# A hybrid RWKV7 / forgetting attention / delta net / differential attention block: score, value and low rank products as pairs of half-array products, and three orders of the out projection

## The chip, the cores and the metric

One core of a Trainium2 chip. The time is that of one execution on the device, in microseconds; of several executions the median is given. A profile is one further execution that the hardware profiler recorded. TensorE multiplies a stationary tile (loaded by a weight load, PEld in the profile) with a moving one (PE); VectorE (DVE), ScalarE (ACT) and GpSimd (POOL) work on vectors, and SyncE (SP) issues transfers.

## The reference, cut to what matters

512 tokens of 2048 features are normalised and multiplied by a wide input matrix. Four mixers of 1024 features each work on parts of the result; their outputs are gated and go through an out projection of 4096 x 2048.

```python
h = rms_norm(x, norm_g[l])
p = jnp.einsum('bsd,dn->bsn', h, w_in[l])
p_rwkv, p_fox, p_gdn, p_diff, z = jnp.split(p, bounds, axis=-1)
y = jnp.concatenate([rwkv7_time_mix(...), forgetting_attention(...),
                     gated_deltanet(...), differential_attention(...)], axis=-1)
x = x + jnp.einsum('bsm,md->bsd', y * jax.nn.silu(z), w_out[l])

# rwkv7_time_mix: the low rank products
w = (w0 + jnp.tanh(w_lo) @ w_up)                 # rank 64
a = jax.nn.sigmoid((a0 + a_lo @ a_up))           # rank 64
# forgetting_attention: 16 heads of 64, by blocks of 128 queries, causal
s = jnp.einsum('bhqd,bhkd->bhqk', q[:, :, q0:q0 + Q_BLOCK], k[:, :, :kv_end]) * scale
s = s + c[:, :, q0:q0 + Q_BLOCK, None] - c[:, :, None, :kv_end]
prob = softmax(where(distance >= 0, s, -inf))
o = jnp.einsum('bhqk,bhkd->bhqd', prob, v[:, :, :kv_end])
# differential_attention: 8 heads with two maps of 64 each, and values of 128
s = jnp.einsum('bhmqd,bhmkd->bhmqk', q[..., q0:q0 + Q_BLOCK, :], k[..., :kv_end, :]) * scale + alibi
weights = prob[:, :, 0] - lam * prob[:, :, 1]
o = jnp.einsum('bhqk,bhkd->bhqd', weights, v[:, :, :kv_end])
```

## The kernel before, in words

Large products are made from F32R parts: every operand is split into a large part and a small rest (`wh` and `wl`, `hh` and `hl`, `gh` and `gl`), and three products (large by large, rest by large, large by rest) add up in one PSUM bank. Smaller products that need full accuracy are F32, for which the trace has two records per product.

The kernel has these stages. First x is normalised, transposed and split (to about 50 us). Then eight steps j run, each on 128 features of every mixer: a stream of weight products (`gemm_fm`, `gemm_tm`, line 66 in the profile, tiles `acc_...`) is the filler, and between its products the mixers' own small products are set in. After the steps come the gate products (`acc_z`), and at the end the out projection (`acc_o`, from line 1394 on).

The order on TensorE is written out: each mixer is a generator (`rwkv_local`, `rwkv_chain`, `gdn`, `inverses`, `fox`, `diff`), and the loop at the end of the stages runs either the next product of the stream or the generator that is due, by an estimated clock `pe[0]`. `MM` (line 60) and `transpose` advance that clock; a generator yields the time that it wants to wait, stretched by `SLACK` = 1.25. `free(tag)` holds a generator back until the clock says that a PSUM bank is free again: `psc` hands out the two banks `sc` of the scores, `ptr` the one bank `tr` of the transposes, each with the time that it is planned to be held. TensorE runs that order strictly; the other engines are ordered by priorities. A bank or an operand that is late therefore stops all of TensorE.

The pieces that the change touches:

- `rwkv_local` (line 552): two F32R products per low rank part: `uh` by `lor` on 128 rows, where the two halves of the rows hold the large part and the rest of `lor`, and `ul` by `lor` on 64 rows. The order is 128 rows, 64, 128, 64, into the banks `pw` and `pa` (two of the tag `sc`).
- `qk_heads` (line 1046) normalises and transposes q and k of a pair of heads (fox) or of maps (diff) and writes three operands: `QS`, for each head both parts of q on the two halves of the rows, `KD`, for each head the large part of k on both halves, and `KL`, the rest of k. That takes six ScalarE and four VectorE instructions on 64 rows.
- `scores` (line 1080) makes per query block and head a 128-row product (QS by KD: large and rest of q with the large part of k in one go) and a 64-row product (QS's large part by KL), of 128, 256, 384 or 512 columns by block. The two heads have banks of their own (`pSf`, `pSd`). In fox a bf16 product with a mask follows per head. Then VectorE adds the bias and takes the maximum (line 1099), and ScalarE exponentiates (line 1101).
- `weighted` in `fox` (line 1140) transposes the weights of one head, copies them (line 1112), waits, and multiplies them with 64 columns of V in F32, into rows 0 to 63 (head 0) or 64 to 127 (head 1) of the bank `po`; then it does the same for the other head. `blocks` (line 1115) puts the scores of a block ahead of the value products of the block before, so that the next scores can follow directly on `po`.
- Two pieces that the change leaves alone show how small tiles run: `rwkv_local` makes `pA` (line 625) of 64-row F32 products, the two row halves in turn, into two banks; `inverses` makes `pm` (from line 1002 on) of products on 32 x 32 tiles, of which the third of each group reads the same rows as the first and writes other columns.
- The out projection: four column blocks `nb` of 512, each in 16 parts; per part 24 products into four banks, token block by token block, each with two groups of three products.

Of the kernel before, what the change touches and what calls it, by code (L numbers as in the profile page):

```python
# [39 lines left out]
# margin on the estimated latencies  # L40
# [11 lines left out]
def hybrid_kernel(ctx: ExitStack, tc: tile.TileContext, ins, out, steps=tuple(range(NJ)), ydbg=None, tail=True):  # L52
# [7 lines left out]
    def MM(o, a, b, **kw):  # L60
        n, m = math.prod(b.shape[1:]), math.prod(a.shape[1:])
        if a.dtype == F32:
            pe[0] += 4 * max(n, m, 32) / 2400
        else:
            pe[0] += max(n, 256 if a.dtype == F32R else 128) / 2400
        return nc.tensor.matmul(o, a, b, **kw)  # L66
# [26 lines left out]
    # banks by use, with the time at which each is expected to be free again  # L93
# [15 lines left out]
    def free(tag, n=1):  # L109
        """Wait until the next n banks are free."""  # L110
        while True:
            b = banks[tag]
            t = max(b[(taken[tag] + i) % len(b)] for i in range(n))
            if t <= pe[0]:
                return
            yield min(t - pe[0], 1.0)
# [6 lines left out]
    def until(*what):  # L123
        """Wait until another thread has come that far."""
        while what not in done:
            yield 0.5
# [18 lines left out]
    # ------------------------------------------------------------ constants  # L145
# [20 lines left out]
    # ------------------------------------------------------------ h = rms_norm(x), transposed, split  # L166
    # with the first product run block of tokens by block of tokens
# [108 lines left out]
    # key minus query position for the last block of queries, with the causal mask; halved for each pair of heads  # L276
# [13 lines left out]
    # ------------------------------------------------------------ streamed products  # L290
# [37 lines left out]
    def gemm_tm(ca, cb, name, evac, need, late=False):  # L328
        """Token-major; with late, the second bank is wanted late."""
# [29 lines left out]
    # ------------------------------------------------------------ low rank parts and gates  # L359
# [4 lines left out]
    # vectors along the features, put on the partitions  # L364
# [35 lines left out]
    # both parts of the low rank products on the two halves of the rows: of the decay's the large one first  # L400
# [33 lines left out]
    # gates: both parts of the weights beside each other  # L434
# [20 lines left out]
    def gates(fab0):  # L455
# [45 lines left out]
        # by block of 32 queries: the sums up to a key within the block, less those from a key up to the block  # L501
# [38 lines left out]
    # ------------------------------------------------------------ RWKV  # L540
# [11 lines left out]
    def rwkv_local(j, res, st):  # L552
# [6 lines left out]
        for i, ps in enumerate(pws):  # L559
            rs = slice(i * C, (i + 1) * C)  # L560
            MM(ps, uh[:, i], lor[i], start=True, stop=False)
            MM(ps, ul[rs], lor[i][rs], start=False, stop=True)
# [31 lines left out]
        # squared norms by token, their reciprocals as row scales  # L594
# [12 lines left out]
        # both halves of the chunks, each as soon as the step before is through with its tiles  # L607
# [3 lines left out]
        for q in range(2):  # L611
# [6 lines left out]
            # decayed interactions within a chunk  # L618
# [22 lines left out]
            # token-major copies  # L641
# [20 lines left out]
        # bonus  # L662
# [12 lines left out]
    def rwkv_chain(j, st, XT):  # L675
# [50 lines left out]
        # group norm by head, gain and offset after the transposition  # L726
# [23 lines left out]
    # ------------------------------------------------------------ gated delta net  # L750
# [12 lines left out]
    def gdn_silu(j, s, a):  # L763
        """Twice the function."""
# [18 lines left out]
    def gdn_local(j, res):  # L783
        # decays within a chunk
# [16 lines left out]
        # k: token-major, norms  # L801
# [24 lines left out]
        # q and the interactions  # L826
# [86 lines left out]
    # ------------------------------------------------------------ unit triangular inverses  # L913
    NB = 48

    def inverses(j, ET, GA, blk, start_rwkv):
# [42 lines left out]
        # the untransposed inverses of the leading blocks  # L959
# [8 lines left out]
        # RWKV: blocks of 32 into 64  # L968
# [16 lines left out]
        # delta net: 32 into 64  # L985
# [27 lines left out]
        # 64 into 128  # L1013
# [13 lines left out]
    # ------------------------------------------------------------ attentions  # L1027
# [18 lines left out]
    def qk_heads(j, ev, kind):  # L1046
# [10 lines left out]
        # by head: both parts of q on the two halves of the rows, the large part of k on both, and its small part  # L1057
        QS = mp.tile([P, 2, T], F32R, name=f"QS{kind}{j}", tag="QS", bufs=1)
        KD = mp.tile([P, 2, T], F32R, name=f"KD{kind}{j}", tag="KD", bufs=1)
        KL = mp.tile([P, T], F32R, name=f"KL{kind}{j}", tag="KL", bufs=1)  # L1060
        halves = slice(0, C), slice(C, P)
        for s, src in enumerate((qa, ka)):
            yield from free("tr")
            pt = ptr(f"pt{kind}{j}_{s}", 8.1)
            for t in range(NT):
                transpose(pt[:, t * P:(t + 1) * P], src[:, t, :])
            for h in range(2):
                hs, other = halves[h], halves[1 - h]
                g = gain[hs, gi + s:gi + s + 1]
                big = (QS, KD)[s][hs, h]  # L1070
                ACT(big, pt[hs], AF.Copy, scale=g)
                if s:
                    ACT(KD[other, h], pt[hs], AF.Copy, scale=g)
                STT(KL[hs] if s else QS[other, h], pt[hs], g, big.bitcast(F32), op0=ALU.mult, op1=ALU.subtract)
            yield 2.0
        yield 4.0
        done.add((kind + "_qk", j))
        return QS, KD, KL

    def scores(qk, qi, name, biases, masked):  # L1080
        """Both halves of a pair: exp of the scores less their maximum, and its sums."""
        QS, KD, KL = qk
        kv = (qi + 1) * P
        yield from free("sc", 2)
        pss = [psc(f"pS{name}_{h}", 3.5 + 0.5 * h) for h in range(2)]
        for h in range(2):
            hs = slice(h * C, (h + 1) * C)
            qs = slice(qi * P, (qi + 1) * P)
            MM(pss[h][:, 0:kv], QS[:, h, qs], KD[:, h, 0:kv], start=True, stop=False)
            MM(pss[h][:, 0:kv], QS[hs, h, qs], KL[hs, 0:kv], start=False, stop=masked)  # L1090
# [14 lines left out]
    def transposed(pr, qi, name):  # L1105
        """In its place."""
# [8 lines left out]
    def blocks(scored, weighted):  # L1115
        """All blocks of queries, the scores of one ahead of the products of the block before."""
# [8 lines left out]
    def fox(j, ev, values, nb):  # L1125
# [14 lines left out]
        def weighted(qi, res):  # L1140
            for h, (pr, _) in enumerate(res):
                yield from transposed(pr, qi, f"f{j}_{qi}_{h}")
                for kt in range(qi + 1):
                    MM(po[h * C:(h + 1) * C, qi * P:(qi + 1) * P], V[:, kt, h * C:(h + 1) * C],
                       pr[:, kt * P:(kt + 1) * P], start=(kt == 0), stop=(kt == qi))
# [56 lines left out]
    # ------------------------------------------------------------ all groups, in the order of an estimated clock  # L1202
# [26 lines left out]
    # those whose gates come in the first step, before their values  # L1229
# [127 lines left out]
    # ------------------------------------------------------------ gating  # L1357
    # the first half goes through DRAM, the second stays where the mixers were
# [35 lines left out]
    # ------------------------------------------------------------ out projection and residual  # L1394
# [6 lines left out]
    for nb in range(D // T):  # L1401
        cs = slice(nb * T, (nb + 1) * T)
        accs = [bank(tag, f"acc_o{nb}_{t}", 0.0) for t, tag in enumerate(sets[nb % 2])]
        for half in range(2):
            for q in halves[half]:
                for gp in (0, 2):
# [7 lines left out]
                    for t in range(NT):  # L1414
                        ts_ = slice(t * P, (t + 1) * P)
                        for g in range(2):
                            m = (gp + g) * NJ + q
                            sl = slice(g * T, (g + 1) * T)
                            MM(accs[t], gh[m][:, ts_], wh[:, sl], start=(first and g == 0), stop=False)
# [35 lines left out]
```

## Time and profile before

| | |
|---|---|
| three runs | 2347.38, 2352.05, 2352.88 us; median 2352.05 |
| span of the profiled execution | 2347.7 us |
| TensorE matmuls | busy 2326.0 us (99%), 14364 records |
| weight loads | busy 1939.0 us (83%) |
| VectorE, ScalarE, GpSimd | busy 1386.2 us (59%), 832.1 us (35%), 220.0 us (9%) |
| mean granted TensorE clock | 0.996 |
| mixers (50 to 1640 us) | 1590 us |
| last gate products (1640 to 1989.5 us) | 349.5 us |
| out projection (1989.5 to 2347.7 us) | 358.2 us |

The profiled execution's own span, 2347.7 us, lies within the three runs and 4.35 us below their median. Matmuls are pipelined and a record's end is modelled, so two records overlap and the sum of their durations is no use of time; what a product costs is read from its start to the start of the next one. In the timeline a row is one record or several alike that follow each other (xcount), with its start and its length; `64*128 64x512` is 64 rows by 128 columns of the array, fed 512 columns.

### The profile page before, as it was taken

The numbers are of one execution on the slowest core, as the hardware profiler recorded it, in microseconds if no ns is written. First come the engines' busy times: TensorE is split into PE (matmuls) and PEld (weight loads), VectorE is DVE, ScalarE is ACT, GpSimd is POOL, SyncE is SP. The second block draws the span as 40 slices with busy tenths as digits, with TensorE's granted clock in tenths as the row PEclk, the third lists the DMA queues.
The fourth block names the chain that finished last, engine by engine and source line by source line (L and its number), as shares of the span: only waits on it lengthen the run. The fifth ranks groups of instructions, "written<-read, shape, count | busy, mean of one in ns | idle before, by whom it ended". The sixth has DMA issues, their size and how long they took to land.

```text
span 2347.7 us, 36745 instructions
## 1 busy us (share of the span) xinstructions
PE 2326.0 (99%) x14364; PEld 1939.0 (83%) x14364; DVE 1386.2 (59%) x3585; ACT 832.1 (35%) x1456; POOL 220.0 (9%) x434
## 2 busy tenths in 40 slices
PE   7999999999999999999999999999999999999999
PEld 6788779779878977987987897798788888888887
DVE  6468487567757847756785784776553343422222
ACT  4234343344344334334434333443332222311111
POOL 2200020102102002010210201201000000100000
PEclk9999999999999999999999999999999999999999
DMA  5433223323322322332332232233354444654452
GB/s 162 101 87 99 81 62 97 88 58 94 97 61 66 102 80 54 104 84 58 99 89 64 69 99 75 60 97 87 96 161 135 129 112 110 175 132 108 117 125 72
DMA packets 320848, 225.78 MB, mean 96 GB/s; under 512 B 16911, under 2 KB 284370, under 8 KB 320162
## 3 DMA queue, kind: packets, MB, share of 16 engines
q1 hardware_dynamic: 298722, 187.05, 30.2%
q0 software_dynamic: 8128, 14.84, 3.1%
q10 hardware_dynamic: 13824, 21.54, 2.8%
q8 instruction: 113, 1.85, 0.3%
q14 instruction: 61, 0.50, 0.1%
HBM read 203.40 MB, written 19.97 MB: 95 GB/s over the span
## 4 chain that ended last, share of the span: by engine, by line
PE 98%; DVE 1%; SPq 0%; DMA 0%; issue 0%; ACT 0%; DVEq 0%; ACTq 0%
PE acc_z L66 15%; PE acc_o L66 15%; PE acc_fqk L66 8%; PE acc_dqk L66 8%; PE acc_vv L66 7%; PE pC L66 5%; PE acc_gk L66 4%; PE acc_k L66 4%; PE acc_gq L66 4%; PE acc_v L66 4%; PE acc_gv L66 4%; PE acc_r L66 4%; PE pSf L66 2%; PE po L66 2%; PE pSd L66 2%; PE pG L66 2%
## 5 line engine op out<-in xcount | busy, mean ns | idle before, releaser
L300 DVE TENSOR_TENSOR wl<-wr,wh 128x1024 fp32r<-128x1024 f32 x318 | 388.9, 1223 | 559.7 <-ACT wh L299 553.3
L299 ACT CAST wh<-wr 128x1024 fp32r<-128x1024 f32 x318 | 333.8, 1050 | 729.8 <-PE acc_o L66 235.1
L66 PE MATMUL acc_z<-hh,wh 128*128 128x512 f32 x512 | 206.8, 404 | 0.0
L66 PE MATMUL acc_z<-hh,wl 128*128 128x512 f32 x512 | 202.4, 395 | 0.0
L66 PE MATMUL acc_z<-hl,wh 128*128 128x512 f32 x512 | 202.4, 395 | 0.0
L66 PE MATMUL acc_o<-wh,gl 128*128 128x512 f32 x512 | 200.9, 392 | 0.0
L66 PE MATMUL acc_o<-wh,gh 128*128 128x512 f32 x512 | 200.6, 392 | 0.0
L66 PE MATMUL acc_o<-wl,gh 128*128 128x512 f32 x512 | 189.4, 392 | 0.0
L66 PE MATMUL acc_fqk<-wh,hh 128*128 128x256 f32 x512 | 136.4, 289 | 0.0
L66 PE MATMUL acc_dqk<-wh,hh 128*128 128x256 f32 x512 | 134.8, 286 | 0.6 <-DVE zt L1235 0.6
L66 PE MATMUL acc_fqk<-wh,hl 128*128 128x256 f32 x512 | 131.3, 279 | 0.0
L66 PE MATMUL acc_dqk<-wh,hl 128*128 128x256 f32 x512 | 131.2, 279 | 0.0
L937 DVE TENSOR_TENSOR bP<-bX,bA 112x2 f32<-112x2 f32 (+30 forms) x248 | 121.9, 492 | 8.2 <-POOL bA L925 2.2
L66 PE MATMUL acc_vv<-wh,hh 128*128 128x256 f32 x448 | 116.5, 283 | 0.0
L66 PEld LDWEIGHTS acc_z<-hh,wl 128*128 128x128 f32 x512 | 96.2, 188 | 23.2
L66 PE MATMUL acc_vv<-wh,hl 128*128 128x256 f32 x448 | 114.8, 279 | 0.0
L66 PEld LDWEIGHTS acc_z<-hh,wh 128*128 128x128 f32 x512 | 96.3, 188 | 22.3 <-issue 0.2
L66 PEld LDWEIGHTS acc_o<-wh,gh 128*128 128x128 f32 x512 | 96.0, 187 | 22.0 <-ACT wh L299 0.3
L66 PEld LDWEIGHTS acc_o<-wh,gl 128*128 128x128 f32 x512 | 96.1, 188 | 21.9
L66 PEld LDWEIGHTS acc_o<-wl,gh 128*128 128x128 f32 x512 | 96.0, 188 | 21.8 <-DVE wl L300 0.3
L66 PEld LDWEIGHTS acc_z<-hl,wh 128*128 128x128 f32 x512 | 96.4, 188 | 20.9
L66 PE MATMUL acc_fqk<-wl,hh 128*128 128x256 f32 x512 | 101.5, 279 | 0.0
(506 smaller groups left out, 5304.1 us busy)
## 6 DMA issues: line engine op xcount, KB each, us to landing
wr<-in_w_in SPq DMA_DIRECT2D x162, 512.0 KB
wr<-in_w_in SPq DMA_DIRECT2D x184, 256.0 KB
wr<-in_w_out SPq DMA_DIRECT2D x64, 512.0 KB
zy<-ydr ACTq DMA_DIRECT2D x30, 256.0 KB
nb<-cdr SPq DMA_DIRECT2D x8, 512.0 KB
xo<-in_x ACTq DMA_DIRECT2D x16, 256.0 KB
gr<-gdr POOLq DMA_DIRECT2D x16, 256.0 KB, 4.4
out<-xo ACTq DMA_DIRECT2D x16, 256.0 KB
```

Of the source, the lines that this page charges most:

```text
L66: return nc.tensor.matmul(o, a, b, **kw)
L299: nc.scalar.copy(wh[:, 0:n], wr[:, 0:n])
L300: TT(wl[:, 0:n], wr[:, 0:n], wh[:, 0:n].bitcast(F32), op=ALU.subtract)
L937: TT(pv_, X[:, 0:n, 0:w], A[:, 0:w, t].unsqueeze(1).to_broadcast([112, n, w]), op=ALU.mult)
```

## The change

The scores become three 64-row products per head instead of a 128-row and a 64-row one, and the two heads take turns: rows 0 to 63 of the array for head 0, rows 64 to 127 for head 1. The operands are then four plain tiles (large part and rest of q and of k), made by two ScalarE and two VectorE instructions on 128 rows. The low rank products are put in the order 128, 128, 64, 64 rows, the last two on the two halves. The value products of fox wait for the transposes of both heads and then take turns between columns 0 to 63 and 64 to 127. The estimated clock is charged half for a product with `side=2`, plus 0.4 for a score visit and 0.2 for a value visit; planned holds of banks and one wait are shortened. In the out projection the column block `nb` = 1 runs its products by group, part and then token block, `nb` = 2 has the two products with `gh` follow each other, and `nb` = 0 and 3 stay as they were. The rest of the diff takes out comments.

```diff
 
-    def MM(o, a, b, **kw):
+    def MM(o, a, b, side=1, **kw):
+
         n, m = math.prod(b.shape[1:]), math.prod(a.shape[1:])
         if a.dtype == F32:
-            pe[0] += 4 * max(n, m, 32) / 2400
+            pe[0] += 4 * max(n, m, 32) / 2400 / side
         else:
-            pe[0] += max(n, 256 if a.dtype == F32R else 128) / 2400
+            pe[0] += max(n, 256 if a.dtype == F32R else 128) / 2400 / side
         return nc.tensor.matmul(o, a, b, **kw)
 
...
         for i, ps in enumerate(pws):
+            MM(ps, uh[:, i], lor[i], start=True, stop=False)
+        for i, ps in enumerate(pws):
             rs = slice(i * C, (i + 1) * C)
-            MM(ps, uh[:, i], lor[i], start=True, stop=False)
-            MM(ps, ul[rs], lor[i][rs], start=False, stop=True)
+            MM(ps, ul[rs], lor[i][rs], side=2, start=False, stop=True)
         lw = lcp.tile([P, T], F32, name=f"lw{j}", tag="lc", bufs=8)
         ACT(lw, pw, AF.Tanh, scale=0.5, bias=w0h[:, j:j + 1])
...
             TT(dv, dv, rv[:, :, s].unsqueeze(3).to_broadcast([P, NT, 2, C]), op=ALU.mult)
         yield 1.2
-        # by head: both parts of q on the two halves of the rows, the large part of k on both, and its small part
-        QS = mp.tile([P, 2, T], F32R, name=f"QS{kind}{j}", tag="QS", bufs=1)
-        KD = mp.tile([P, 2, T], F32R, name=f"KD{kind}{j}", tag="KD", bufs=1)
-        KL = mp.tile([P, T], F32R, name=f"KL{kind}{j}", tag="KL", bufs=1)
-        halves = slice(0, C), slice(C, P)
+
+        parts = []
         for s, src in enumerate((qa, ka)):
+            big, small = [mp.tile([P, T], F32R, name=f"{'QK'[s]}{n}{kind}{j}", tag=f"{'QK'[s]}{n}", bufs=1)
+                          for n in "hl"]
             yield from free("tr")
-            pt = ptr(f"pt{kind}{j}_{s}", 8.1)
+            pt = ptr(f"pt{kind}{j}_{s}", 3.0)
             for t in range(NT):
                 transpose(pt[:, t * P:(t + 1) * P], src[:, t, :])
-            for h in range(2):
-                hs, other = halves[h], halves[1 - h]
-                g = gain[hs, gi + s:gi + s + 1]
-                big = (QS, KD)[s][hs, h]
-                ACT(big, pt[hs], AF.Copy, scale=g)
-                if s:
-                    ACT(KD[other, h], pt[hs], AF.Copy, scale=g)
-                STT(KL[hs] if s else QS[other, h], pt[hs], g, big.bitcast(F32), op0=ALU.mult, op1=ALU.subtract)
+            g = gain[:, gi + s:gi + s + 1]
+            ACT(big, pt, AF.Copy, scale=g)
+            STT(small, pt, g, big.bitcast(F32), op0=ALU.mult, op1=ALU.subtract)
+            parts += [big, small]
             yield 2.0
-        yield 4.0
+        yield 2.0
         done.add((kind + "_qk", j))
-        return QS, KD, KL
+        return parts
 
     def scores(qk, qi, name, biases, masked):
-        """Both halves of a pair: exp of the scores less their maximum, and its sums."""
-        QS, KD, KL = qk
+
+        Qh, Ql, Kh, Kl = qk
         kv = (qi + 1) * P
         yield from free("sc", 2)
-        pss = [psc(f"pS{name}_{h}", 3.5 + 0.5 * h) for h in range(2)]
-        for h in range(2):
-            hs = slice(h * C, (h + 1) * C)
-            qs = slice(qi * P, (qi + 1) * P)
-            MM(pss[h][:, 0:kv], QS[:, h, qs], KD[:, h, 0:kv], start=True, stop=False)
-            MM(pss[h][:, 0:kv], QS[hs, h, qs], KL[hs, 0:kv], start=False, stop=masked)
+        pss = [psc(f"pS{name}_{h}", 3.0 + 0.5 * h) for h in range(2)]
+        qs = slice(qi * P, (qi + 1) * P)
+
+        for i, (a, b) in enumerate(((Qh, Kh), (Ql, Kh), (Qh, Kl))):
+            for h in range(2):
+                hs = slice(h * C, (h + 1) * C)
+                MM(pss[h][:, 0:kv], a[hs, qs], b[hs, 0:kv], side=2, start=(i == 0), stop=(masked and i == 2))
+        pe[0] += 0.4
         res = []
         for h in range(2):
             ps = pss[h]
...
                 yield from transposed(pr, qi, f"f{j}_{qi}_{h}")
-                for kt in range(qi + 1):
+
+            for kt in range(qi + 1):
+                for h, (pr, _) in enumerate(res):
                     MM(po[h * C:(h + 1) * C, qi * P:(qi + 1) * P], V[:, kt, h * C:(h + 1) * C],
-                       pr[:, kt * P:(kt + 1) * P], start=(kt == 0), stop=(kt == qi))
+                       pr[:, kt * P:(kt + 1) * P], side=2, start=(kt == 0), stop=(kt == qi))
+            pe[0] += 0.2
 
         yield from blocks(scored, weighted)
...
-                    for t in range(NT):
-                        ts_ = slice(t * P, (t + 1) * P)
-                        for g in range(2):
-                            m = (gp + g) * NJ + q
-                            sl = slice(g * T, (g + 1) * T)
-                            MM(accs[t], gh[m][:, ts_], wh[:, sl], start=(first and g == 0), stop=False)
-                            MM(accs[t], gl[m][:, ts_], wh[:, sl], start=False, stop=False)
-                            MM(accs[t], gh[m][:, ts_], wl[:, sl], start=False, stop=(last and g == 1))
+                    parts = ((gh, wh), (gl, wh), (gh, wl))
+                    if nb == 2:
+                        parts = ((gh, wh), (gh, wl), (gl, wh))
+                    order = [(t, g, i) for t in range(NT) for g in range(2) for i in range(3)]
+                    if nb == 1:
+                        order.sort(key=lambda o: (o[1], o[2], o[0]))
+                    for t, g, i in order:
+                        a, b = parts[i]
+                        MM(accs[t], a[(gp + g) * NJ + q][:, t * P:(t + 1) * P], b[:, g * T:(g + 1) * T],
+                           start=(first and g == 0 and i == 0), stop=(last and g == 1 and i == 2))
         for t in range(NT):
             band(PRIO_EVAC)
             xo = op_a.tile([P, T], F32, name=f"xo{nb}_{t}", tag="xo", bufs=6)
```

## Rows read from the trace of the kernel before

**Rows 1.** The page: busy time, share, instructions by engine; last chain by engine.
```profile
PE 2326.0 (99%) x14364; PEld 1939.0 (83%) x14364; DVE 1386.2 (59%) x3585; ACT 832.1 (35%) x1456; POOL 220.0 (9%) x434
...
PE 98%; DVE 1%; SPq 0%; DMA 0%; issue 0%; ACT 0%; DVEq 0%; ACTq 0%
```

**Rows 2.** Waits of TensorE: who waited for whom, us in total, times, longest.
```profile
PE ph L70 <- DVE x L228: 12.1, 2, 10.8
...
PE acc_lora L66 <- ACT V L1224: 0.8, 1, 0.8
...
PE acc_vv L66 <- DVE hl L236: 0.2, 1, 0.2
```

**Rows 3.** Busy time by stretch (stretch, its us, each engine, clock, DMA): the mixers.
```profile
50.00:1640.00 1590.00, 1587.69 (x10986) 1339.10 (x10985) 1096.37 (x3126) 627.63 (x1187) 195.23 (x389) 0.99 0.31 82
```

**Rows 4.** The chain in order of time (start us, us, what): two plain runs.
```profile
1742.49 247.10 PE acc_z L66 x1059
1989.58 353.66 PE acc_o L66 x1536
```

**Rows 5.** Timeline of TensorE (start us, us, what): a score visit, 512 columns.
```profile
725.52 0.48 PE L66 MATMUL pSd<-KDdiff,QSdiff 128*128 128x512 f32 x1
725.93 0.50 PE L66 MATMUL pSd<-KLdiff,QSdiff 64*128 64x512 f32 x1
...
727.22 0.45 PE L66 MATMUL pC<-ZV,ET 128*64 128x64 f32 x4
```

**Rows 6.** Timeline: score visits of 128, 256 and 384 columns, first and next.
```profile
691.55 0.22 PE L66 MATMUL pSd<-KDdiff,QSdiff 128*128 128x128 f32 x1
...
692.46 0.50 PE L66 MATMUL acc_gv<-hh,wh 128*128 128x512 f32 x1
...
607.66 0.28 PE L66 MATMUL pSf<-KDfox,QSfox 128*128 128x256 f32 x1
...
608.80 0.29 PE L66 MATMUL pSf<-negm_q,identb 128*128 128x128 bf16 x2
...
1012.85 0.43 PE L66 MATMUL po<-prf,V 128*64 128x128 f32 x2
1013.21 0.45 PE L66 MATMUL pSf<-KDfox,QSfox 128*128 128x384 f32 x1
...
1014.70 0.28 PE L66 MATMUL pSf<-negm_q,identb 128*128 128x128 bf16 x2
```

**Rows 7.** Timeline: sixteen records of 64-row products in turn, and the next.
```profile
706.77 1.16 PE L66 MATMUL pA<-AR,BK 64*128 64x128 f32 x16
707.86 0.49 PE L66 MATMUL pd<-V,prd 128*128 128x128 f32 x2
```

**Rows 8.** Timeline of a value visit; its weight loads (ns least, median, most).
```profile
261.17 1.09 PE L66 MATMUL po<-prf,V 128*64 128x128 f32 x8
262.19 0.66 PE L70 MATMUL pPf<-ident,prf 128*128 128x128 f32 x4
...
L66 PEld LDWEIGHTS po<-prf,V x320: 132/137/137, 223.2 to 1643.3; 128*64 128x64 f32 x160
```

**Rows 9.** Timeline: the first three products on 32 x 32 tiles.
```profile
262.77 0.22 PE L66 MATMUL pm<-GA,Gg 32*32 32x32 f32 x2
262.78 0.21 PE L66 MATMUL pm<-Gg,GA 32*32 32x32 f32 x1
```

**Rows 10.** Timeline: low rank products of one step, first and what follows.
```profile
679.63 0.40 PE L66 MATMUL pw<-lor,uh 128*128 128x512 f32 x1
...
681.24 0.33 PE L70 MATMUL ptdiff<-ident,kadiff 128*128 128x128 f32 x1
```

**Rows 11.** Groups by line and shape (xcount, busy us, mean ns, idle before): operands.
```profile
L1074 DVE SCALAR_TENSOR_TENSOR KLdiff<-ptdiff,gain,KDdiff 64x512 fp32r<-64x512 f32 x16 | 12.0, 750 | 1.5 <-ACT KDdiff L1073 1.0
```

**Rows 12.** Busy time by stretch: two stretches of a lower granted clock.
```profile
699.50:702.90 3.40, 3.40 (x10) 2.36 (x11) 1.52 (x9) 1.25 (x5) 0.00 (x0) 0.50 0.54 150
1488.00:1491.40 3.40, 3.40 (x11) 2.26 (x10) 1.67 (x7) 0.95 (x4) 0.00 (x0) 0.50 0.36 107
```

## What I expect of the change

> **What bounds the kernel now.** I read the page first. TensorE's matmul row stands at 99% of the span, and the chain that ended last is 98% TensorE [rows 1]. The waits of TensorE come next: there are eight, 17.1 us in all, the longest at the very start (x still to be normalised) and none above 0.8 us behind the first product run [rows 2]. So TensorE works through one queue without holes, and any time it no longer needs comes off the end, as long as no other engine gets late. In the stretch of the mixers VectorE is busy 1096 of 1590 us [rows 3], so there is room, but not endless room.
>
> A busy TensorE is not one that streams all the time. Products of 512 columns in plain runs start 247.10/1059 = 0.233 us apart in the gate products and 353.66/1536 = 0.230 us apart in the out projection [rows 4]. In the score products of the last query block, also 512 columns wide, the starts lie 0.41 to 0.43 us apart [rows 5]. These alternate between 128 rows of the array (QS with KD) and 64 rows (QS with KL). Each change of the array's shape thus costs about 0.43 - 0.235 = 0.195 us. This is the price on which most of the sum rests: it is a drain before the change and an uncovered weight load behind it.
>
> **The scores.** There are 8 steps x 2 kinds (fox, diff) x 4 query blocks = 64 visits. Before, a visit is four products in turn (128, 64, 128, 64 rows), so four changes of shape, the one back to 128 rows at its end included. From the first start to that of what follows it takes 0.91, 1.14 and 1.49 us for the blocks of 128, 256 and 384 columns [rows 6] and 1.70 us for 512 [rows 5]. With four streams and three and a half changes each (a drain before a first load counts half, and the third of these visits comes out of a 64-column shape and has four) the first three streams come out at 0.06, 0.117 and 0.177 us. The last visit follows a two-record F32 product, behind which a start is recorded early; its stream I take as 0.235, from the plain runs.
>
> After, a visit is six 64-row products, rows 0 to 63 and rows 64 to 127 in turn, with two changes of shape. Whether the two halves run beside each other the trace shows for another tile: pA's products are 64-row, alternate in the same way and write two banks. Sixteen records of 128 columns (an F32 product is two records) take 1.09 us from the first start to the next instruction's [rows 7]. A single F32 record of 128 columns takes 0.11 us: a visit of po with eight lasts 1.02 us to the next start, one with two 0.36 [rows 6, 8], so six take 0.66. In turn the sixteen would take 1.76 us. Less 0.195 us for load and drain, 0.90 us are left for eight pairs, 0.112 us a pair. I take F32R halves to behave alike.
> - Two changes fewer: 64 x 2 x 0.195 = 25.0 us.
> - 23 visits start straight behind po or pC, in a 64-column shape (the 384-column one shown behind po [rows 6] is one of them). They lose a third change, because there is no way back to 128 rows first: 23 x 0.195 = 4.5 us.
> - Streams: four of each width, 4 x (0.06 + 0.117 + 0.177 + 0.235) = 2.36 us, become three pairs, the smallest held at pA's 0.112: 3 x (0.112 + 0.117 + 0.177 + 0.235) = 1.92 us. Times 16: 7.0 us.
> Together 36.5 us. If the halves ran one after another, streams would be six: 3.53 us, and the gain 25.0 + 4.5 - 18.7 = 10.8 us.
>
> **Fox's value products.** They are 128x64 and F32. Before, each of the two heads of a query block is a visit of its own, behind its own transposes: 64 visits, 320 records. After, one visit per block with the heads in turn, on output columns 0 to 63 and 64 to 127.
> - 32 round trips of shape go. Of the visit's 1.02 us, 1.02 - 8 x 0.11 = 0.14 us are its own drain and first load; the drain ahead of it (0.09, half a change) and the load behind it (0.05 to 0.15) make 0.28 to 0.38. I take 0.33, the middle: 10.6 us (9.0 to 12.2).
> - Streams: 320 x 0.11 = 35.2 us become 160 x 0.112 = 17.9 us, 17.3 us less, if column halves overlap. The nearest rows are pm's: its third product reads the same rows 32 to 63 as the first, writes other columns, and starts 0.01 us behind it, while the first alone streams for 0.11 x 32/128 = 0.027 us [rows 9]. These tiles are 32 wide and not 64, so this is likely and not shown.
> Together 27.9 us.
>
> [...]
>
> **Low rank products.** Per step four products become two full ones and a pair. Before they take 1.61 us from first start to next [rows 10]. After: 2 x 0.233 + 0.09 + 0.233 + 0.10 + 0.09 = 0.98 us. Times 8: 5.0 us (3.1 if the pair runs in turn).
>
> **Edits that I cost at nothing.** Building the operands takes two ScalarE and two VectorE instructions per head pair and kind instead of six and four, each of the same 512 elements per partition, 0.750 us for VectorE's [rows 11]: 16 x 2 x 0.75 = 24 us off VectorE, beside TensorE's work, worth nothing now. It offsets the 4% faster pace that the mixers ask of VectorE. The bank of the transposes is planned free 3.0 instead of 8.1 us later; one conversion and one subtraction, some 1.5 us, must be through by then, and if they aren't, the next transposes on TensorE's queue wait, and all products behind them. The planner's clock charged a head pair's scores 4 x 1408/2400 = 2.35 us where they took about 5.3; it will charge 1.76 + 1.6 = 3.36 against some 3.0. The margin that it had by accident goes. Its other charge for products (512/2400 = 0.213 for 0.233) remains as cover.
>
> The out projection keeps its 1536 products and its order in the first and last column block. In the second, four token blocks take turns; in the third, two products in a row have the same stationary tile. The gate products already have that (wh twice running) and are no faster: 0.233 against 0.230 [rows 4]. I take 0. Bounds for 768 products: -7.7 us if they came down to 0.22, the time of two F32 records (2 x 0.11 [rows 8]), +2.3 us at the gate products' pace. No bank or DMA queue is passed over by this.
>
> [...]
>
> **The sum.** 36.5 + 27.9 + 5.0 = 69.4 us. The profiled span is 2347.7 us; 2347.7 - 69.4 = 2278.3. The median of the runs, 2352.05, is 4.35 above that span, so 2283.
>
> **Rivals.**
> - Column halves run in turn: 17.3 us missing, 2300. For it: no row shows 64-wide pairs over all 128 rows. Against: pm. [...]
> - F32R row halves run in turn: 25.7 us missing in the scores and 1.9 in the low rank products, 2311. For it: every paired product in the trace is F32. Against: KL's shape change costs what pA's does.
> - Neither overlaps: 2283 + 17.3 + 27.6 = 2328.
> - The gain is handed back as waits: the planner's margin goes, and TensorE stands before transposes whose bank is not free. The nearest wait is the 0.8 us of the first product behind the first run [rows 2]; one such in each of the 32 visits of the operands' transposes: 26 us, 2309. Against: TensorE is idle for 2.3 us of the mixers' 1590 now [rows 3].
> - Slower: in F32R every alternation between row halves is itself a change of shape. A score visit then has seven changes instead of four: 64 x 3 x 0.195 = 37.4 us lost, streams 18.7 lost, 4.5 kept; the low rank products keep 1.6 and po 27.9. Net +22 us, 2374. It decides from (10.8 + 27.9 + 3.1)/328 alternations = 0.127 us each; in pA they lie inside 0.112 us a pair.
>
> **How the numbers follow.** Forecast 0.67; column halves in turn 0.10; F32R halves in turn 0.08; waits 0.07; neither 0.04; slower 0.04. The range goes from 2269 (clock and out projection both at their good ends, 2283 - 14.5) to 2312, past the two rivals in which one kind of halves runs in turn and the waits as priced: 0.67 + 0.10 + 0.08 + 0.05 = 0.90, of which some is lost to what is not listed. 0.3% (7 us) is what can be told from no change here. Faster 0.94, same 0.02 (waits of 60 us), slower 0.04.
>
> **What would show it.** In the changed profile's timeline a score visit of 512 columns is three pairs some 0.233 us apart, two starts nearly together, about 0.9 us from first start to next; if it is 1.5 us, the halves run in turn; above 2 us, the slower rival. A po visit of four key blocks takes 16 records in about 1.1 us; 1.9 us means in turn. The low rank visit is about 1.0 us. The mixers' stretch shortens by some 69 us, the out projection stays at 354 us. TensorE's waits stay below 5 us after the start; a new row there, on transposes or scores, would be the handing back. Wrong at the root would be a stretch without shape changes that got slower.

## The result, and the profile after

The changed kernel takes 2282.3 us in the median of four runs (2281.42 to 2282.59) against 2350.11 us for the kernel before beside it (2347.38 to 2352.88): a ratio of 0.9714, 95% interval 0.9701 to 0.9728. The forecast was 2283. The profiled span went from 2347.7 to 2279.6 us.

The page of the changed kernel: busy time by engine, and the last chain by engine.

```profile
PE 2251.7 (99%) x14492; PEld 1899.4 (83%) x14492; DVE 1341.7 (59%) x3553; ACT 781.0 (34%) x1392; POOL 214.7 (9%) x434
...
PE 86%; issue 6%; POOL 3%; DMA 3%; DVE 2%; ACT 1%; SPq 0%; POOLq 0%; ACTq 0%; DVEq 0%
```

There are 128 records more (64 visits of six products instead of four) and 74 us less busy time. TensorE still stands at 99%, but the chain is no longer 98% TensorE as in [rows 1]: it now leaves it at a few places. Where, the waits of TensorE say (who for whom, us in total, times, longest):

```profile
PE ph L71 <- DVE x L229: 12.0, 2, 10.8
PE pC L67 <- DVE rs L695: 4.1, 7, 0.8
...
PE acc_vv L67 <- POOL w0l L243: 1.2, 1, 1.2
PE acc_vv L67 <- DVE hl L237: 1.1, 1, 1.1
PE acc_lora L67 <- ACT V L1226: 0.8, 1, 0.8
```

The first and the last are old [rows 2]; those of `acc_vv` lie in the first 50 us and were shorter before. The second is new: in seven steps, the second product of a link of the RWKV recurrence (`pC<-rs`) waits for VectorE's copy `rs`. More on it below. From 50 us on, all waits together are 6.0 us, against 2.3 before.

The share of the chain that lies off TensorE (14%) is not time lost. One of the seven waits, in the chain in order of time:

```profile
489.46 16.52 issue
506.00 5.00 DMA GA<-gcd
511.17 7.31 POOL GA L797 x16
...
521.06 0.20 DVE rs L695
521.30 0.44 PE pC L67 x4
```

Behind a wait of 0.33 us the chain is followed back over other engines for some 33 us, and TensorE worked through all of these but the 0.33.

Busy time by stretch: the mixers, and the out projection.

```profile
50.00:1572.00 1522.00, 1516.20 (x11067) 1301.90 (x11068) 1054.49 (x3096) 579.56 (x1126) 190.13 (x389) 1.00 0.32 85
1921.00:2279.60 358.60, 354.01 (x1538) 288.02 (x1536) 101.28 (x100) 76.73 (x81) 9.67 (x18) 1.00 0.49 121
```

The mixers took 1590 us before [rows 3] and take 1522 now, so all 68 us come from there. The out projection takes 358 us as before.

Timeline of TensorE in the changed kernel: score visits of 512 and of 128 columns, the value visit of four key blocks, the low rank products, each with what follows.

```profile
1051.29 0.50 PE L67 MATMUL pSd<-Khdiff,Qhdiff 64*128 64x512 f32 x2
1051.63 0.40 PE L67 MATMUL pSd<-Khdiff,Qldiff 64*128 64x512 f32 x2
1051.86 0.40 PE L67 MATMUL pSd<-Kldiff,Qhdiff 64*128 64x512 f32 x2
1052.19 0.27 PE L67 MATMUL pC<-rs,ET 64*64 64x64 f32 x1
...
1026.97 0.33 PE L67 MATMUL pSd<-Khdiff,Qhdiff 64*128 64x128 f32 x2
...
1027.45 0.38 PE L67 MATMUL pC<-Sb,AR 128*128 128x128 f32 x1
...
1005.65 1.09 PE L67 MATMUL po<-prf,V 128*64 128x128 f32 x16
1006.67 0.32 PE L67 MATMUL pC<-ZV,ET 64*64 64x64 f32 x2
...
1039.66 0.39 PE L67 MATMUL pw<-lor,uh 128*128 128x512 f32 x1
1039.89 0.39 PE L67 MATMUL pa<-lor,uh 128*128 128x512 f32 x1
1040.21 0.50 PE L67 MATMUL pw<-lor,ul 64*128 64x512 f32 x1
1040.21 0.50 PE L67 MATMUL pa<-lor,ul 64*128 64x512 f32 x1
1040.64 0.38 PE L67 MATMUL pG<-gY,KTs 128*128 128x128 f32 x1
```

A 512-column score visit lasts 0.90 us from first start to next instead of 1.70 [rows 5]: 0.34 us for the first pair with its weight load, 0.23 for the second, 0.33 for the third with the drain behind it. The 128-column visit lasts 0.48 instead of 0.91 [rows 6]. The sixteen records of a value visit take 1.02 us, as long as eight did [rows 8]. The low rank products take 0.98 us instead of 1.61 [rows 10], and the two of 64 rows start in the same hundredth of a microsecond.

Adding up, over all records, the time from each product's start to that of the next one, by what the product writes: the scores with fox's mask products went from 87.6 to 45.5 us, the value products from 44.2 to 22.3, the low rank products from 12.9 to 7.8, the out projection from 353.4 to 353.7, the gate products 364.3 to 364.2. Some 4 us of the scores' 42 moved to the product ahead of a visit, which now has the drain: 41 of the 64 visits came out of a 128-row, 128-column shape before and had none ahead of them, and a 512-column product ahead of a visit now lasts 0.327 us to the next start instead of 0.231.

The changes of shape can be counted. Over all records in order of start, the rows and columns of the array differ from those of the record before 895 times in the kernel before and 664 times in the changed one: 231 fewer, as many as the forecast's terms take away together (128 and 23 in the scores, 64 in the value products, 16 in the low rank products).

The granted clock, in stretches of both kernels (the kernel before, then the changed one):

```profile
88.50:91.90 3.40, 3.40 (x9) 2.35 (x8) 0.46 (x3) 0.25 (x1) 0.00 (x0) 0.50 0.12 36
...
85.40:92.20 6.80, 5.94 (x27) 4.36 (x26) 1.70 (x8) 0.25 (x1) 0.00 (x0) 0.50 0.27 77
```

From 50 us on, the kernel before has five stretches at 0.50, 3.4 us each: the four of which [rows 12] shows two, and this early one. Inside them 512-column products start 0.43 us apart (701.25, 701.68 and 702.10 us) and not 0.233. Such a stretch is priced at half its length from here on, 1.7 us, which is an estimate; by these starts it would be 1.55. The changed kernel has the early one alone, 6.8 us long in the profiled execution.

### The profile page after: what moved, and what is told of

Same layout as the page of the kernel before. It is cut to its first block, busy times and chain, and to the rows that moved or that the text cites. A ratio compares the mean times of both kernels' runs of the same rounds, so it can differ in the third digit from the quotient of the medians.

```text
span 2279.6 us, 36867 instructions
## 1 busy us (share of the span) xinstructions
PE 2251.7 (99%) x14492; PEld 1899.4 (83%) x14492; DVE 1341.7 (59%) x3553; ACT 781.0 (34%) x1392; POOL 214.7 (9%) x434
## 4 chain that ended last, share of the span: by engine, by line
PE 86%; issue 6%; POOL 3%; DMA 3%; DVE 2%; ACT 1%; SPq 0%; POOLq 0%; ACTq 0%; DVEq 0%
PE acc_z L67 16%; PE acc_o L67 14%; PE acc_fqk L67 8%; PE acc_dqk L67 8%; PE acc_vv L67 7%; PE acc_k L67 4%; PE acc_v L67 4%; PE acc_r L67 4%; PE acc_gv L67 3%; PE pC L67 3%; POOL GA L797 2%; PE acc_gq L67 2%; DMA GA<-gcd 2%; PE pm L67 1%; PE pSf L67 1%
## 5 line engine op out<-in xcount | busy, mean ns | idle before, releaser
L67 PE MATMUL acc_o<-wh,gl 128*128 128x512 f32 x512 | 185.3, 392 | 0.0
L67 PE MATMUL acc_o<-wl,gh 128*128 128x512 f32 x512 | 179.2, 392 | 0.0
L67 PE MATMUL acc_o<-wh,gh 128*128 128x512 f32 x512 | 177.8, 392 | 0.2 <-ACT wh L300 0.2
L67 PEld LDWEIGHTS acc_o<-wh,gh 128*128 128x128 f32 x512 | 96.1, 188 | 22.3 <-ACT wh L300 0.6
```

## The experiments

**Only the scores changed.** The kernel before, with the new `qk_heads` and `scores`.

```diff
-            MM(pss[h][:, 0:kv], QS[:, h, qs], KD[:, h, 0:kv], start=True, stop=False)
-            MM(pss[h][:, 0:kv], QS[hs, h, qs], KL[hs, 0:kv], start=False, stop=masked)
+        for i, (a, b) in enumerate(((Qh, Kh), (Ql, Kh), (Qh, Kl))):
+            for h in range(2):
+                MM(pss[h][:, 0:kv], a[hs, qs], b[hs, 0:kv], side=2, start=(i == 0), stop=(masked and i == 2))
```

> The kernel before with only the new operands and paired scores (and their charge on the planner's clock). Theory of the sum: scores are worth 36.5 us by themselves, so some 2314 us against 2350.5. Rival, that the parts are not additive and the new order as a whole carries the gain: clearly less than 30 us here, with waits of TensorE in the profile that the full change does not have. Score visits of 512 columns should take 0.90 us from first start to next.

Measured: 2318.68 us against 2348.08, ratio 0.9871 (0.9857 to 0.9886). That is 29.4 us, 7 less than the sum's 36.5. The starts of the score products sum to 45.5 us, exactly as in the full change, so the term itself is there; the trace has 5.9 us of waits in the mixers that the kernel before does not have, the largest of them

```profile
PE pC L67 <- ACT yt L723: 3.0, 8, 0.5
```

and 1.3, 0.9 and 0.7 us on three others. The shape changes 761 times, 134 fewer than before where the term takes away 151: so 17 came in elsewhere, 3.3 us at 0.195 each. Against these stands the clock: none of the four later stretches at 0.50 is left in this trace, at 1.7 us each up to 6.8 us to the good. 36.5 + 6.8 - 5.9 - 3.3 = 34.1 us, and the profiled spans differ by 2347.7 - 2316.0 = 31.7, so some 2 us stay open.

**Only the value products changed.** The kernel before, with the new `weighted`.

```diff
+            for kt in range(qi + 1):
+                for h, (pr, _) in enumerate(res):
+                    MM(po[...], V[:, kt, ...], pr[...], side=2, start=(kt == 0), stop=(kt == qi))
```

> The kernel before with only fox's value products in one visit per block, heads in turn. Theory of the sum: 10.6 us for 32 round trips of the array's shape and 17.3 us for overlapping column halves, 27.9 us in all, some 2322 us. Rival (column halves in turn): 10.6 us, some 2340. Rival (not additive): less than 20 us with waits in the profile.

Measured: 2341.65 us against 2348.08, ratio 0.9968 (0.9956 to 0.9981): 6.4 us, where 27.9 were expected. The value products' starts sum to 22.3 us as in the full change. The time by itself would fit column halves in turn (2340), but these starts rule that out. What happened is the rival of the handed-back gain, as the waits of TensorE show:

```profile
PE pC L67 <- DVE rs L694: 10.1, 11, 2.0
PE pgo L71 <- ACT gsqk L773: 3.7, 6, 0.6
PE pG L67 <- ACT gY L872: 3.7, 6, 0.6
```

That is 17.5 us in three rows that the kernel before has not got.

**The same, with a longer planned wait.** The planner sets the recurrence's second product in 1.4 (times `SLACK`) after the first; this makes it 2.2.

```diff
-            yield 1.4
+            yield 2.2
             rs = mp.tile([C, P], F32, name=f"rs{j}_{c}", tag="rs", bufs=1)
```

> The kernel before with fox's value products in one visit and, on top, the planned wait ahead of the recurrence's second product raised from 1.4 to 2.2. The value products alone gave 8 us at the clock though their own starts shrank by 21.9 us; the profile showed 10.1 us of new waits of that product on VectorE, and 7.4 us of two others on ScalarE. If the missing gain is the waits, those 10 us come back: some 2331 us. If instead the value products cost something elsewhere (streams, weight loads), the waits go and the time stays near 2340.

Measured: 2323.89 us against 2349.07, ratio 0.9897 (0.988 to 0.9914): 25.2 us, where 6.4 were gained without the longer wait. More than the 10 us of the one row came back, because all three rows above are gone; the longest wait in the mixers is now

```profile
PE acc_dqk L67 <- DVE zt L1239: 1.0, 1, 1.0
```

So the missing gain was the waits, and one number in the planner removed them. The 25.2 us are not the price of the value products alone. This trace has none of the four later stretches at 0.50 (with the early one longer, about 5 us to the good), 3 us more waits than the kernel before, and 55 fewer changes of shape where the term takes away 64 (1.8 us). The profiled spans differ by 2347.7 - 2321.1 = 26.6 us; with these three taken out the value products come to about 26 us, an estimate from the two traces. The kernel before with the longer wait alone was not run.

**The changed kernel, scores head by head.** Head 0's three products, then head 1's.

```diff
-        for i, (a, b) in enumerate(((Qh, Kh), (Ql, Kh), (Qh, Kl))):
-            for h in range(2):
+        for h in range(2):
+            for i, (a, b) in enumerate(((Qh, Kh), (Ql, Kh), (Qh, Kl))):
```

> The changed kernel, but a score visit runs head 0's three products and then head 1's three: the same six products, the same two changes of shape and the same planner's order; only the alternation goes. If the overlap of the row halves carries the streams, at most one pair still overlaps, and five streams take the place of three: 16 x (5 x 0.59 - 1.92) = 16 us more than the changed kernel's 2282, so about 2298; 26 us more (2308) if none overlaps. Rival, that the gain is the shape changes alone and the overlap adds nothing: 2282 again.

Measured: 2282.05 us, ratio 0.9716 (0.9702 to 0.9731); the same as the changed kernel. By what was written down, this spoke for shape changes alone. The timeline of the visit shows that it does not:

```profile
1051.49 0.51 PE L67 MATMUL pSd<-Khdiff,Qhdiff 64*128 64x512 f32 x2
1051.83 0.40 PE L67 MATMUL pSd<-Khdiff,Qldiff 64*128 64x512 f32 x2
1052.07 0.39 PE L67 MATMUL pSd<-Kldiff,Qhdiff 64*128 64x512 f32 x2
1052.39 0.27 PE L67 MATMUL pC<-rs,ET 64*64 64x64 f32 x1
```

In the program Kh,Qh of head 1 comes after Kl,Qh of head 0. In the trace the two Kh,Qh start together, then the two Kh,Ql, then the two Kl,Qh: TensorE started head 1's first product beside head 0's first, while head 0's second and third still stood in line. The overlap is there without the alternation, so this run could not take it away; the next does.

**The changed kernel, both heads on one half.** Head 1 gets head 0's operands; its own scores are left out.

```diff
-                hs = slice(h * C, (h + 1) * C)
+                hs = slice(0, C)
                 MM(pss[h][:, 0:kv], a[hs, qs], b[hs, 0:kv], side=2, ...)
```

> The changed kernel, but all six products of a score visit use rows 0 to 63, so head 1 gets head 0's scores again: head 1's scores are left out. Same columns, same banks, same shape, same order; only nothing can run beside anything. If the row halves overlap in the changed kernel, six streams take the place of three: 16 x (6 x 0.59 - 1.92) = 26 us more, some 2308, and a visit of 512 columns takes 1.6 us instead of 0.90. If the score gain is shape changes alone: 2282 and 0.90.

Measured: 2312.3 us against 2349.07, ratio 0.9845 (0.983 to 0.9859): 30.0 us more than the changed kernel. The 512-column visit:

```profile
1070.60 0.73 PE L67 MATMUL pSd<-Khdiff,Qhdiff 64*128 64x512 f32 x2
1071.17 0.62 PE L67 MATMUL pSd<-Khdiff,Qldiff 64*128 64x512 f32 x2
1071.63 0.63 PE L67 MATMUL pSd<-Kldiff,Qhdiff 64*128 64x512 f32 x2
1072.19 0.33 PE L67 MATMUL pC<-rs,ET 64*64 64x64 f32 x2
```

It takes 1.59 us, six streams of 0.233 and 0.19 for the changes of shape. F32R row halves do overlap, and without that the change would be worth 30 us less. The 4 us above the expected 26 come from the smallest width: there six products on one half take 0.81 us with the changes of shape, so 0.10 each and not the 0.06 that the forecast read off products with a change of shape behind each.

**The changed kernel, values head by head.**

```diff
-            for kt in range(qi + 1):
-                for h, (pr, _) in enumerate(res):
+            for h, (pr, _) in enumerate(res):
+                for kt in range(qi + 1):
```

> The changed kernel, but a value visit runs all products of head 0 and then all of head 1: same products, same single visit, no alternation. If the overlap of column halves is worth 17.3 us, nearly all of that goes (one record per visit can still overlap): 14 to 17 us more than 2282, so 2296 to 2299. Rival, that the round trips of shape are the whole gain: 2282 again.

Measured: 2288.35 us, ratio 0.9742 (0.9727 to 0.9756): 6.1 us more than the changed kernel, between the two theories. The visits of three and of four key blocks:

```profile
1185.54 1.14 PE L67 MATMUL po<-prf,V 128*64 128x128 f32 x12
1186.62 0.50 PE L67 MATMUL acc_r<-hh,wh 128*128 128x512 f32 x1
...
1010.17 1.58 PE L67 MATMUL po<-prf,V 128*64 128x128 f32 x16
1011.68 0.33 PE L67 MATMUL pC<-ZV,ET 64*64 64x64 f32 x2
```

They last 1.08 and 1.51 us; in turn they last 0.81 and 1.02. The visits of one and two key blocks stay within 0.01 us of theirs (0.37 and 0.59). 8 x (0.27 + 0.49) = 6.1 us is the whole difference. Column halves overlap too, and again past the program's order, but not without limit: with six records of head 0 in front, 0.27/0.11 = 2.4 records are lost, with eight 4.4. Both leave 3.6: as if about four records could be passed, an estimate from these two visits.

**The changed kernel, values by twos.** Two key blocks (four records) of one head, then two of the other.

```diff
+            for k0 in range(0, qi + 1, 2):
+                for h, (pr, _) in enumerate(res):
+                    for kt in range(k0, min(k0 + 2, qi + 1)):
```

> The changed kernel, but a value visit takes two key blocks of head 0, then two of head 1, and so on. Head by head, visits of two and four records per head stayed as short as in turn, those of six and eight got 0.27 and 0.49 us longer: as if some four records of one half could be stood behind the other half's. If so, groups of four records cost nothing: 2282 within 1.5 us, a visit of eight records per head stays at 1.02 to 1.10 us. If alternation itself counts, the visits of six and eight records are about as long as head by head (1.07 and 1.51 us) and the time is 2286 to 2289.

Measured: 2282.7 us, ratio 0.9718 (0.9703 to 0.9732). The visit of four key blocks:

```profile
1006.70 1.15 PE L67 MATMUL po<-prf,V 128*64 128x128 f32 x16
1007.77 0.33 PE L67 MATMUL pC<-ZV,ET 64*64 64x64 f32 x2
```

1.07 us, half a record more than in turn. That agrees with the reading of about four records.

**The changed kernel with the old charges on the planner's clock.**

```diff
-            pe[0] += 4 * max(n, m, 32) / 2400 / side
+            pe[0] += 4 * max(n, m, 32) / 2400
...
-        pe[0] += 0.4
...
-            pe[0] += 0.2
```

> The changed kernel with the planner's clock charged in full for the paired products and without the 0.4 and 0.2 per visit, so the small products are set in at other places of the stream. The changed kernel has 4.1 us of new waits, one per step in seven steps, of the recurrence's second product on VectorE's copy. If the new charges brought those waits, they go here and the time falls by 4 to 7 us (2276 to 2278); if they come from the changed sequence itself, the time stays within 3 us of 2282 and the waits are there, at this or another place.

Measured: 2282.54 us, ratio 0.9717 (0.9702 to 0.9731). The waits on `rs` are there:

```profile
PE pC L67 <- DVE rs L695: 5.6, 7, 1.5
```

The new charges did not bring them. What did, the new products or the shortened holds and waits of the planner, this run does not tell apart, since it keeps both.

**The changed kernel with one order in the out projection.**

```diff
-                    if nb == 2:
-                        parts = ((gh, wh), (gh, wl), (gl, wh))
...
-                    if nb == 1:
-                        order.sort(key=lambda o: (o[1], o[2], o[0]))
```

> The changed kernel with the out projection in the order of before in all four column blocks. Theory: the order is worth nothing, 2282 within 2 us, and each column block's 384 products start 0.230 us apart as they do in the three orders of the changed kernel. Rival: one of the two new orders hides a gain or a loss of up to 8 us, and the time moves by that.

Measured: 2283.55 us, ratio 0.9719 (0.9703 to 0.9735). Busy time in the stretch of the out projection:

```profile
1924.00:2282.00 358.00, 353.66 (x1535) 287.22 (x1533) 101.65 (x100) 76.30 (x81) 9.67 (x18) 1.00 0.48 121
```

358 us again. The three orders are worth the same: neither alternating four banks nor repeating a stationary tile matters here.

**The changed kernel with the longer planned wait.** The same edit as for the values alone.

> The changed kernel with the planned wait ahead of the recurrence's second product raised from 1.4 to 2.2, so that about four more stream products stand before it. If the seven waits on VectorE's copy are a product placed too early, they vanish and the time falls by 4 to 6 us, to some 2277. Rival: VectorE's copy sits behind a blocked instruction in its own queue whatever TensorE does, or the recurrence gets long enough to hold something else: no gain, 2282, and waits elsewhere.

Measured: 2278.02 us (2277.57 to 2279.59), ratio 0.9699 (0.9684 to 0.9713). The changed kernel itself ran 2281.42 to 2282.59, with one out order 2282.14 to 2283.87 and with the old charges 2281.80 to 2283.01; the ranges do not touch. TensorE's waits in it:

```profile
PE acc_lora L67 <- ACT V L1226: 0.8, 1, 0.8
...
PE acc_dqk L67 <- DVE zt L1237: 0.2, 1, 0.2
```

The row of `rs` is gone, and this version beats both kernels, the changed one by some 4 us. The seven waits' 4.1 us are not all of it: between the profiled spans, 3.6 us apart, the first 50 us also have 2.7 us less of waits and the early stretch at 0.50 is 3.4 us shorter, while the shape changes 687 times, 23 more than in the changed kernel (4.5 us at 0.195 each).

Why the copy was late is in the timeline of the changed kernel, ahead of the wait that ends at 333.39 us:

```profile
329.88 0.44 PE L67 MATMUL pC<-ZV,ET 64*64 64x64 f32 x4
329.93 0.17 DVE L158 TENSOR_TENSOR rsq_go<-rsq_go,rsh_go 128x4 f32<-128x4 f32 x1
331.77 0.69 DVE L769 SCALAR_TENSOR_TENSOR gc_k<-gt_k,gc_k 128x512 f32<-128x512 f32 x1 [1.68 <-ACT gt_k L768]
332.39 0.41 DVE L617 TENSOR_TENSOR AR<-kk,E 128x256 f32<-128x256 f32 x1
332.73 0.41 DVE L618 TENSOR_TENSOR AR<-rw_r,E 128x256 f32<-128x256 f32 x1
333.06 0.27 DVE L695 COPY rs<-pC 64x128 f32<-64x128 f32 x1
...
333.39 0.44 PE L67 MATMUL pC<-rs,ET 64*64 64x64 f32 x4 [0.78 <-DVE rs L695]
```

VectorE was idle for 1.68 us, for most of them with the copy ready to run (its product had started at 329.88 and took 0.44). It did not take the copy first: in front of `rs` stood a step of the delta net that waited for ScalarE, which in turn waited for GpSimd, and two more instructions (L617, L618). That is a place in the sequence, not a lack of time.

## Why the prediction was right, point by point

- **What bounds the kernel.** Right. All of the gain is in the mixers and came off the end.
- **The price of a change of shape, 0.195 us.** Right. It carried over to products that the trace had not shown: the 512-column visit on one half is six streams of 0.233 and 0.19 us. The uncovered load is in the trace of the kernel before: in a 512-column score visit the second, third and fourth load start in the same hundredth of a microsecond as their own products (725.93, 726.36 and 726.79 us), after 0.24 to 0.25 us without a load. In the changed kernel's visit the loads of the second and third pair start 0.23 us ahead of their products.
- **The scores, 36.5 us.** Right in size: 42 us less from start to start, of which 4 moved to the products ahead. The split was also right: with nothing to overlap the change loses 30 us. Two sizes inside were off. A 128-column pair takes 0.48 - 0.195 = 0.29/3 = 0.10 us and not pA's 0.112, and a single one in turn takes 0.10 and not 0.06, so the rival "F32R halves in turn" was priced 4 us too low.
- **The value products, 27.9 us.** Right in size: their own starts shrank by 21.9 us, and the run with the longer wait comes to about 26 once clock, waits and changes of shape elsewhere are taken out. The step that was marked as not shown, overlap of 64-column halves over the same rows, holds: sixteen records in 1.02 us.
- **Low rank products, 5.0 us.** 0.98 us a visit, as worked out; this part was not run alone.
- **Out projection, 0.** Right, and the run with one order isolates it.
- **The clock, 0.** Right within the 6.8 us that the range counts for its good end. No run shows that figure: it is the estimate of 1.7 us for each of four stretches, and the starts of the products inside them give 1.55 each, 6.2 us. The four stretches of which [rows 12] shows two have no successor, but the early one, which the forecast did not count, was 3.4 us longer in the profiled execution: 6.8 - 1.7 = 5.1 us to the good by that estimate. The traces of the single parts tell more: with the scores alone none of the four is left, with the value products alone one, at another place (1312.1 to 1315.5 us). Why the clock fell there, no run shows.
- **Waits below 5 us.** Missed narrowly: 6.0 us from 50 us on, 3.7 more than before, of which the new row has 4.1, and at another place than named. The first 50 us have 2.5 us more as well, which varies between executions (0.2 in the run with the scores head by head). The forecast looked at the bank of the transposes; what got late was a copy of the recurrence behind a blocked instruction on VectorE. It also took the margin on the planner's clock for the point of danger, and the run with the old charges has the same waits.
- **That the parts add up.** This held for what the products take and not for the time. Scores alone and values alone gave 29.4 and 6.4 us; with 5.0 for the low rank products that is 40.8, not 67.8. Each single part shifts the sequence into waits of its own (5.9 and 17.5 us in their traces) and into changes of shape elsewhere (17 and 5 more than its terms say), and the full change, by where its products fall, into 4.1 us and none. A chance of 0.07 for waits that eat a third of the gain was low for a planner whose order is fixed by estimates: one of the two parts by itself lost three quarters that way. The forecast met 2283 with a sum whose terms were right, and by luck with two effects that it had put at nothing and that cancelled: 69.4 + 5.1 (clock) - 6.2 (waits, 3.7 and 2.5) = 68.3 us, against 68.1 between the profiled spans.

Value products on the same 128 rows and different columns run beside each other, loads included: in a visit of four key blocks in the changed kernel sixteen loads of 0.137 us each lie within 0.85 us, and the sixteen records take 1.02.

## What to carry to other kernels

Where TensorE is the bound, count its changes of shape in the trace and price them: here 0.195 us each, nearly the 0.233 us of a 512-column product. Products of half the rows or half the columns should stand together, both halves at once (here in banks of their own where they split the rows; a shared bank was not tried); strict alternation was not needed here so long as only a few products of one half stood in front of the other (three score products or four value records cost nothing, six and eight value records 0.27 and 0.49 us a visit). After such a change look at the waits, the clock and the changes of shape elsewhere before judging it: with an order fixed by estimated times, a part measured as 6 us until one planned wait was longer, and then as 25.

## What the runs showed of the hardware that was not expected

In these runs TensorE did not start all its products in the order of the program; where the description of the kernel before says that it runs that order strictly, they do not bear it out. Products for one half of the array passed products that stood in line for the other half, in F32R by row halves (head by head, both heads' first products start together at 1051.49 us, though head 0's second and third, at 1051.83 and 1052.07, stand ahead of head 1's; visit unchanged at 0.90 us) and in F32 by column halves (visits of 0.37 and 0.59 us unchanged, later ones 0.27 and 0.49 us longer). The reach worked out from the value visits is about four records, an estimate; for the scores, with three products in front, no limit was met. A late operand did stop TensorE: in the changed kernel for up to 0.8 us behind `rs`, 4.1 us in seven waits, and with only the value products changed for up to 2.0 us, 10.1 us in eleven.
